# An encoder layer's output projection: its steps issued in the program's order on every engine, with outputs, gates and C stored by chunk

## The chip, the cores and the metric

The kernel runs on one core of one Trainium2 chip. The metric is the time of one execution in microseconds (us), and the median of several executions is what is compared: 2937.86 us before, from three runs between 2935.85 and 2945.36 us.

## What is computed

One layer of a bidirectional encoder in float32, for two sequences of 1024 and 2048 tokens with 1024 features each. An RMS norm and an input projection feed a Fourier group (512 features) and a bidirectional state-space group (1536 features, in chunks of 128 tokens). Each has a SiLU gate. The state-space outputs are normalised in four groups of 384 features, all 2048 features pass one output projection, and the residual is added:

```
y_s = y_s * jax.nn.silu(z_s)
yg = y_s.reshape(b, s, N_BC_GROUPS, D_SSM // N_BC_GROUPS)
yg = yg * lax.rsqrt(jnp.mean(yg * yg, axis=-1, keepdims=True) + EPS)
y_s = yg.reshape(b, s, D_SSM) * ssd_norm_w
h = h + jnp.concatenate([y_f, y_s], axis=-1) @ w_out
h = h + (p @ w_ple_in) * jax.nn.sigmoid(h @ w_ple_gate)
```

A final RMS norm closes the layer. The change touches the output projection (`h + ... @ w_out`) and the group norm ahead of it.

## The kernel before

Four phases follow one another. The first, the input projection with the state-space part, takes about two thirds of the span; its order is written out by hand. The second does the Fourier group, the third the output projection, the fourth the gated embedding and the last norm. The order of the last three is made by a scheduler that lists the instructions of all engines ahead of time.

The 3072 tokens are three blocks of eight chunks of 128 tokens (P, S1, S2). The first two phases leave their outputs in device memory: `Yd`, for each block 16 rows of 128 features by 1024 tokens; `ZSd`, the gates of block S1; `CTd`, its matrices C. In these arrays the tokens of one feature lie together, so that the rows of one chunk are 512 B pieces.

The output projection takes 24 steps: twelve pairs of chunks for the first 1024 of the 2048 features (p = 0, rows 0 to 7 of `Yd`), then the same twelve for the others (p = 1). The partial result goes to `Hd` in between. A step is a Strassen-Winograd product: 256 tokens by 1024 features times 1024 by 1024 weights as seven products P1 to P7 of quarter size. The left operands are A11, A12, A22, S1, S2, S3, S4, sums and differences of quarters of `y` (`halves`, lines 1066 to 1097: `s1`, `s2`, `s3` and last `s4`). Each operand is split into a high part `ah` (ACT, a cast, L1074) and a low part `al` (DVE, a subtraction, L1075); each product is twelve matmuls of 512 columns (L1104). P1, P6 and P7 accumulate one after another in the same PSUM bank X; after each of them ACT copies the bank to a buffer `pu` (L1113; the copies are called p1, u2, u3). P2 writes bank Y, P5 and P3 bank Z, P4 bank W. DVE adds banks Y, Z and W to the residual `ht` (L1218), POOL adds the copies (L1219). Weights come from `WSd`, 1 MB for each product and each half of the features, and are split like the operands (`product_weights`, L858 on ACT, L859 on DVE).

Ahead of that stands the preparation of a step (`prepare`): the loads of `y` (SyncE); in steps 4 to 7 and 16 to 19, whose chunks are in block S1, a correction for the backward state (matmuls `po` L1185, products on DVE L1186, sums on POOL L1190); squares on ACT (L865) and their sums `rs` on POOL (L866, L867) for each chunk; the split of `rs` into `sh` (ACT L871, POOL L872); two matmuls `pb` that add over the features (L874); Ln and Exp on ACT, each after a table load (L875, L876); and the scaling of `y` on POOL (L880). The program writes down the preparation of step n+2, then the scaling and operands of step n+1, then the products of step n, and the scheduler interleaves them.

## Time and profile before

| what | value |
|---|---|
| median of three runs | 2937.86 us |
| the profiled execution | 2937.68 us |
| its span, first to last instruction | 2935.9 us |
| mean granted TensorE clock | 0.983 |
| mean DMA rate | 150 GB/s |

The profile is that of one execution. Busy time is given for TensorE's matmuls (PE) and weight loads (PEld), VectorE (DVE), ScalarE (ACT) and GpSimd (POOL); SP is SyncE, which issues DMAs. A group's row has its line, engine, operation, tiles (out<-in) and count, then the busy time in us and the mean in ns, then the engine's idle time just before and who ended it. A row of the timeline has a start and a duration in us; a bracket at its end has the idle time before it and what ended that. Matmuls overlap in the pipeline, so their durations are longer than the distance between their starts. A wait for several events is put down to the one that came last.

### The profile page before, as it was taken

The numbers are of one execution on the slowest core, as the hardware profiler recorded it, in microseconds if no ns is written. First come the engines' busy times: TensorE is split into PE (matmuls) and PEld (weight loads), VectorE is DVE, ScalarE is ACT, GpSimd is POOL, SyncE is SP. The second block draws the span as 40 slices with busy tenths as digits, with TensorE's granted clock in tenths as the row PEclk, the third lists the DMA queues.
The fourth block names the chain that finished last, engine by engine and source line by source line (L and its number), as shares of the span: only waits on it lengthen the run. The fifth ranks groups of instructions, "written<-read, shape, count | busy, mean of one in ns | idle before, by whom it ended". The sixth has DMA issues, their size and how long they took to land.

```text
span 2935.9 us, 46306 instructions
## 1 busy us (share of the span) xinstructions
PE 2806.0 (96%) x17206; PEld 2550.2 (87%) x17206; DVE 2148.7 (73%) x3364; ACT 1454.0 (50%) x3008; POOL 1497.0 (51%) x1091
## 2 busy tenths in 40 slices
PE   6999999999999999999999999788998899989998
PEld 6999999999999999999999999776776677768887
DVE  3787777687778686778787776796767876776665
ACT  4545465443545564445444444345555645555554
POOL 1255656542567777643656655455777577610000
PEclk9999999999999999999999999889999999999999
DMA  3244565462465665544455554466453654451221
GB/s 96 88 146 150 166 187 166 125 185 79 127 192 165 200 189 159 160 123 117 144 161 157 154 159 132 151 231 227 144 173 127 229 167 141 158 198 67 96 96 63
DMA packets 327997, 440.09 MB, mean 150 GB/s; under 512 B 19824, under 2 KB 250932, under 8 KB 323932
## 3 DMA queue, kind: packets, MB, share of 16 engines
q1 hardware_dynamic: 327484, 436.08, 47.1%
q8 instruction: 136, 2.23, 0.3%
q10 hardware_dynamic: 288, 1.05, 0.1%
q14 instruction: 89, 0.73, 0.1%
HBM read 328.41 MB, written 109.71 MB: 149 GB/s over the span
## 4 chain that ended last, share of the span: by engine, by line
PE 73%; DVE 7%; POOL 6%; issue 5%; DMA 5%; ACT 4%; SPq 0%; POOLq 0%; DVEq 0%; ACTq 0%
PE ps L361 41%; PE X L1104 7%; PE Z L1104 4%; PE po L648 4%; PE pst L606 3%; PE pd L574 3%; PE W L1297 2%; PE Y L1104 2%; DMA y<-Yd 2%; PE ptt L421 1%; DVE s L1080 1%; DVE al L1075 1%; PE W L1104 1%; PE pr L1028 1%; POOL wl L190 1%
## 5 line engine op out<-in xcount | busy, mean ns | idle before, releaser
L361 PE MATMUL ps<-uh,wh 128*128 128x342 f32 (+1 forms) x2880 | 955.8, 332 | 11.4 <-ACT uh L267 8.2
L361 PE MATMUL ps<-ul,wh 128*128 128x342 f32 (+1 forms) x2880 | 920.6, 320 | 2.5 <-DVE ul L268 2.5
L361 PE MATMUL ps<-uh,wl 128*128 128x342 f32 (+1 forms) x2880 | 922.2, 320 | 0.4 <-POOL wl L190 0.4
L190 POOL TENSOR_TENSOR wl<-wr,wh 128x1024 fp32r<-128x1024 f32 x120 | 296.4, 2470 | 659.3 <-ACT wh L189 658.1
L361 PEld LDWEIGHTS ps<-uh,wh 128*128 128x128 f32 x2880 | 545.6, 189 | 35.0 <-issue 15.8
L361 PEld LDWEIGHTS ps<-ul,wh 128*128 128x128 f32 x2880 | 548.5, 190 | 4.2 <-DVE ul L268 3.5
L361 PEld LDWEIGHTS ps<-uh,wl 128*128 128x128 f32 x2880 | 545.1, 189 | 1.2 <-POOL wl L190 1.1
L558 ACT ACTIVATE R<-R,lb 128x128 f32<-128x128 f32 x1152 | 352.8, 392 | 16.9 <-POOL R L549 16.9
L549 POOL TENSOR_SCALAR_AFFINE_SELECT R<-R 128x512 f32<-128x512 f32 x288 | 275.7, 980 | 6.8 <-DMA R<-ROWd 6.8
L586 POOL TENSOR_TENSOR xw<-xm,wd 128x512 f32<-128x512 f32 x144 | 189.5, 1327 | 136.3 <-ACT xm L423 110.8
L617 DVE SCALAR_TENSOR_TENSOR H<-H,cd,pst 128x64 f32<-128x64 f32 x888 | 182.6, 274 | 102.2 <-PE pst L606 100.0
L367 ACT COPY raw<-ps 128x342 f32<-128x342 f32 x180 | 79.1, 439 | 340.6 <-PE ps L361 339.7
L1104 PE MATMUL X<-whP,ah 128*128 128x512 f32 x480 | 196.7, 410 | 14.1 <-ACT pu L1113 8.4
L402 DVE SCALAR_TENSOR_TENSOR xT<-raw,cvt,xT 128x1024 f32<-128x1024 f32 x144 | 195.5, 1358 | 2.6
L1104 PE MATMUL X<-wlP,ah 128*128 128x512 f32 x480 | 194.5, 405 | 1.6 <-DVE wlP L859 1.6
L1104 PE MATMUL X<-whP,al 128*128 128x512 f32 x480 | 193.6, 403 | 2.4 <-DVE al L1075 2.4
L1219 POOL TENSOR_TENSOR ht<-ht,pu 128x512 f32<-128x512 f32 x96 | 150.4, 1578 | 72.3 <-ACT pu L1113 46.6
L652 DVE TENSOR_TENSOR y<-y,yt 128x512 f32<-128x512 f32 (+1 forms) x144 | 161.4, 1121 | 5.0
L272 ACT ACTIVATE zT<-ps 128x342 f32<-128x342 f32 (+1 forms) x108 | 49.1, 455 | 220.7 <-PE ps L361 220.4
L1075 DVE TENSOR_TENSOR al<-s,ah 128x512 fp32r<-128x512 f32 x144 | 137.7, 981 | 26.5 <-ACT ah L1074 26.0
L565 DVE TENSOR_TENSOR R<-R,cb 128x512 f32<-128x512 f32 x144 | 148.5, 1031 | 5.0
L651 DVE TENSOR_TENSOR yt<-po,er 128x512 f32<-128x512 f32 (+1 forms) x144 | 91.2, 633 | 75.9 <-PE po L648 67.7
(266 smaller groups left out, 5772.8 us busy)
## 6 DMA issues: line engine op xcount, KB each, us to landing
R<-ROWd SPq DMA_DIRECT2D x144, 512.0 KB
wr<-in_w_in SPq DMA_DIRECT2D x120, 512.0 KB
er<-EXPd SPq DMA_DIRECT2D x144, 256.0 KB
Hd<-ht SPq DMA_DIRECT2D x48, 512.0 KB
ht<-Hd SPq DMA_DIRECT2D x48, 512.0 KB
y<-Yd SPq DMA_DIRECT2D x46, 512.0 KB
wlP<-WSd SPq DMA_DIRECT2D x21, 1024.0 KB
Yd<-y SPq DMA_DIRECT2D x72, 256.0 KB
```

What stands on the lines that cost most here:

```text
L190: G.tensor_tensor(wl, raw, wh.bitcast(F32), op=ALU.subtract)
L361: T.matmul(ps[:, :n], lhsT=wt[:, kt, :], rhs=ut[:, kt, :n], start=(i == 0), stop=(i == 3 * KT - 1))
L402: V.scalar_tensor_tensor(dst, raw[:, k:k + TB], cvt[:, 20 * k + ct:20 * k + ct + 1], dst, op0=ALU.mult, op1=ALU.add)
L549: G.affine_select(out=R, in_=R, pattern=[[0, 2], [0, 2], [sgn, P]], compare_op=ALU.is_ge, fill=NEG, base=0, channel_multiplier=-sgn)
L558: S.activation(R[:, h, d, c, :], R[:, h, d, c, :], AF.Exp, bias=self.B.lb[:, 2 * p + c, hc + h:hc + h + 1])
L565: V.tensor_tensor(E[0], E[0], cb.unsqueeze(1).broadcast_to([P, 2, 2 * P]), op=ALU.mult)
L586: G.tensor_tensor(xw, self.xm[c4].rearrange("p c (h e) -> p c h e", h=2), col(self.B.wd[:, c4:c4 + 4, hc:hc + 2]).broadcast_to([P, 4, 2, 6 ...
L617: V.scalar_tensor_tensor(dst[:, e], H[d][:, cc, e], B.cd[:, cc, hc + h:hc + h + 1], pst[:, c, e], op0=ALU.mult, op1=ALU.add)
L652: V.tensor_tensor(y[:, cr], y[:, cr], t[:, cr], op=ALU.add)
L1075: V.tensor_tensor(al, src, ah.bitcast(F32), op=ALU.subtract)
L1104: T.matmul(ps, lhsT=at[:, k, :], rhs=wt[:, k, :], start=(first and i == 0), stop=(i == 11), skip_group_check=not first)
L1219: return lambda t: G.tensor_tensor(h, h, t, op=ALU.add)
```

## The change

Four things change.

- `Yd`, `ZSd` and `CTd` are laid out by chunk: the rows of one chunk lie together. A load of `y` for one chunk is then 4 KB in one piece for each partition, not eight of 512 B; the stores by the first two phases, for several chunks at a time, are in pieces of 512 B, not of 2 or 4 KB.
- The preparation and the products are cut into the small methods of a class `Step`, and a function `run(n)` writes them down in a fixed order: the products of step n (`c`), between them the roots, scaling and operands of step n+1 (`d`), and the loads, corrections, squares and the split of the sums of step n+2 (`e`). For runs 1 to 22 the scheduler is off: every engine takes its instructions in the order of the program. Runs 0 and 23, the preparation of step 1 and all else stay with the scheduler.
- `big`, the buffer of the correction, is taken anew for each corrected step; before, one was kept throughout.
- In run 11, the last of the first half, the weights of the second half are asked for after each product and split at fixed places (`weights_asked`, `weights_parted`). Before, `product_weights` stood behind the step.

The diff, cut to its core (lines left out are marked):

```diff
-    Yd = [dram.tile([P, 16, TB], F32, name=f"Yd{i}") for i in range(3)]
...
-    ZSd = dram.tile([P, NU, TB], F32, name="ZSd")
-    CTd = dram.tile([P, NG, TB], F32, name="CTd")
+    ZSd = dram.tile([P, NCH, NU, P], F32, name="ZSd")
+    CTd = dram.tile([P, NCH, NG, P], F32, name="CTd")
...
-                        pre(s_ + 9, nc.sync.dma_start, CTd[:, i, :], CT)
+                        pre(s_ + 9, nc.sync.dma_start, CTd[:, :, i, :], CT.rearrange("p (c l) -> p c l", l=P))
...
-                nc.sync.dma_start(Yd[self.B.bi][:, unit_place(self.u), tk], self.y[c4].rearrange("p c l -> p (c l)"))
+                cs = slice(c4, c4 + 4)
+                nc.sync.dma_start(Yd[self.B.bi][:, cs, unit_place(self.u), :], self.y[c4])
                 if self.B.b["n"] == "S1":
-                    nc.sync.dma_start(ZSd[:, self.u, tk], self.zT[:, tk])
+                    nc.sync.dma_start(ZSd[:, cs, self.u, :], self.zT[:, tk].rearrange("p (c l) -> p c l", l=P))
...
-    def group_rstd(sh, pb, rs):
+    def group_parts(sh, rs):
         S.copy(sh[:, 0], rs)
         G.tensor_tensor(sh[:, 1], rs, sh[:, 0].bitcast(F32), op=ALU.subtract)
+    def group_rstd(sh, pb, rs):
         for j in range(2):
             T.matmul(pb, lhsT=ones_r, rhs=sh[:, j], start=(j == 0), stop=(j == 1))
         S.activation(rs, pb, AF.Ln, bias=eps4, scale=1.0 / 384.0)
@@ -938,7 +941,7 @@
...
-        first_y = [Yd[0][:, 0:8, q * P:q * P + P] for q in range(2)]
+        first_y = [Yd[0][:, q, 0:8, :] for q in range(2)]
...
-                    Yd[seq + q][:, fourier_place(f), :], yv[:, q * TB:(q + 1) * TB])
+                    Yd[seq + q][:, :, fourier_place(f), :], yv[:, q * TB:(q + 1) * TB].rearrange("p (c l) -> p c l", l=P))
...
-        def prepare(p, i):
...
+        steps = [(p, i) for p in range(2) for i in range(NP)]
...
+        class Step:
...
-                    nc.sync.dma_start(y, Yd[bi][:, 8 * p:8 * p + 8, tk])
+                    nc.sync.dma_start(y, Yd[bi][:, c, 8 * p:8 * p + 8, :])
...
+                        nc.sync.dma_start(self.big[:, q, 0:2, :], CTd[:, c, 2 * p:2 * p + 2, :])
+                        nc.sync.dma_start(self.big[:, q, 2:8, :], ZSd[:, c, 6 * p:6 * p + 6, :])
...
+            def correct(self, q):
...
+                for g in range(2):
+                    po = mps.tile([P, 3, P], F32, tag="sm", bufs=3, name="po")
+                    for j in range(3):
+                        T.matmul(po[:, j, :], lhsT=hbs[-1][:, 3 * g + j, :], rhs=ct[:, g, :], start=True, stop=True)
+                    V.tensor_tensor(zb[:, 3 * g:3 * g + 3, :], po, zb[:, 3 * g:3 * g + 3, :], op=ALU.mult)
+                ssd = self.ys[q].rearrange("p (r k) l -> p r k l", r=2)[:, :, 1:4, :]
+                G.tensor_tensor(ssd, ssd, zb.rearrange("p (r k) l -> p r k l", r=2), op=ALU.add)
...
+            def squared(self, q):
...
+                squares(self.ys[q], sq, self.rss[q])
+            def summed(self):
+                self.sh = yp.tile([P, 2, 4, P], F32R, tag="sh", bufs=1, name="sh")
+                group_parts(self.sh, self.rs)
+            def rooted(self):
                 pb = mps.tile([P, 4, P], F32, tag="sm", bufs=3, name="pb")
-                group_rstd(sh, pb, rs)
-            def rest():
-                for q in range(2):
-                    if rss:
-                        group_scale(ys[q], rss[q])
-                    bi, c = todo[2 * i + q]
+                group_rstd(self.sh, pb, self.rs)
+            def scaled(self, q):
+                if not self.first:
+                    group_scale(self.ys[q], self.rss[q])
...
+            def operand(self, k):
+                a11, a12, a21, a22 = (self.ys[q][:, 4 * r:4 * r + 4, :] for q in range(2) for r in range(2))
+                if k == 0:
+                    self.two("A11", a11)
+                    self.diff("s3", a11, a21, ALU.subtract)
+                elif k == 1:
+                    self.diff("s1", a21, a22, ALU.add)
+                    self.two("A12", a12)
+                elif k == 2:
+                    self.diff("s2", self.s1, a11, ALU.subtract)
+                    self.two("S2", self.s2)
+                elif k == 3:
+                    self.two("S1", self.s1)
+                elif k == 4:
+                    self.two("S3", self.s3)
+                elif k == 5:
+                    self.two("A22", a22)
+                elif "S4" not in self.A:
+                    self.diff("s4", a12, self.s2, ALU.subtract)
+                    self.two("S4", self.s4)
+            def add(self, q, ns, ps):
+                h = self.hts[q][:, ns]
                 V.tensor_tensor(h, ps, h, op=ALU.add)
-                return lambda t: G.tensor_tensor(h, h, t, op=ALU.add)
+            def plus(self, q, ns, t):
+                h = self.hts[q][:, ns]
+                G.tensor_tensor(h, h, t, op=ALU.add)
+            def stored(self):
...
+        def weights_parted(w):
...
+        def run(n, newer=None):
...
+            c.operand(6)
+            product(X, c.A, W_, "A11", "P1")
+            if d is not None and not d.first and n:
+                d.rooted()
             p1 = kept(X)
-            product(Y, A, W, "A12", "P2")
-            add(0, N0, Y)(p1)
-            product(X, A, W, "S2", "P6", first=False)
+            if e is not None:
+                if steps[n + 2] == (1, 0):
+                    incoming(1)
+                e.rows()
+            if d is not None:
+                d.scaled(0)
+                d.scaled(1)
+            product(Y, c.A, W_, "A12", "P2")
+            asked(0)
+            c.add(0, N0, Y)
+            c.plus(0, N0, p1)
+            if b is not None:
+                b.stored()
+            product(X, c.A, W_, "S2", "P6", first=False)
+            asked(1)
             u2 = kept(X)
-            product(Z, A, W, "S1", "P5")
-            more = add(1, N1, Z)
-            product(X, A, W, "S3", "P7", first=False)
+            if d is not None:
+                d.operand(0)
+            product(Z, c.A, W_, "S1", "P5")
+            asked(2)
+            c.add(1, N1, Z)
+            if d is not None:
+                d.operand(1)
+                d.operand(2)
+            if e is not None:
+                e.correct(0)
+            parted(0)
+            product(X, c.A, W_, "S3", "P7", first=False)
+            asked(3)
             u3 = kept(X)
-            more(u3)
-            product(X2, A, W, "A22", "P4")
-            add(1, N0, X2)(u3)
-            product(Z, A, W, "S4", "P3", first=False)
-            add(0, N1, Z)(u2)
-            for q, (bi, c) in enumerate(todo[2 * i:2 * i + 2]):
-                nc.sync.dma_start(Hd[bi * NCH + c], hts[q])
-        ready = prepare(0, 0)()
+            c.plus(1, N1, u3)
+            if e is not None:
+                e.correct(1)
+                e.squared(0)
+            if d is not None:
+                d.operand(3)
+            parted(1)
+            product(X2, c.A, W_, "A22", "P4")
+            asked(4)
+            c.add(1, N0, X2)
+            c.plus(1, N0, u3)
+            if d is not None:
+                d.residuals()
+                d.operand(4)
+            if e is not None:
+                e.squared(1)
+            parted(2)
+            product(Z, c.A, W_, "S4", "P3", first=False)
+            asked(5)
+            c.add(0, N1, Z)
+            if e is not None:
+                e.summed()
+            if d is not None:
+                d.operand(5)
+            c.plus(0, N1, u2)
+            parted(3)
+            if newer is not None:
+                asked(6)
+                for k in range(4, 7):
+                    parted(k)
+                W.update(new)
+        all_[0].rows()
+        for k in range(7):
+            all_[0].operand(k)
+        all_[0].residuals()
         ld = product_weights(0, NAMES[3:4], W)
         with tc.issue_after(ld.ins):
-            coming = prepare(0, 1)
+            all_[1].rows()
+        for q in range(2):
+            all_[1].squared(q)
+        all_[1].summed()
+        all_[1].rooted()
         ld = product_weights(0, NAMES[4:], W)
         with tc.issue_after(ld.ins):
             incoming(0)
-        steps = [(p, i) for p in range(2) for i in range(NP)]
-        for n, (p, i) in enumerate(steps):
-            cur, after = ready, coming
-            with tc.issue_after(ld.ins):
-                if n + 2 < len(steps):
-                    if steps[n + 2] == (1, 0):
-                        incoming(1)
-                    coming = prepare(*steps[n + 2])
-                if n + 1 < len(steps):
-                    ready = after()
-                else:
-                    ph.close()
-                    q4 = ctx.enter_context(tc.tile_pool(name="q4", bufs=1, **R_))
-                    ready = turned(0)
-            outputs(i, W, *cur)
-            if i == NP - 1:
-                W = {}
-                last_w = product_weights(p + 1, NAMES, W)
+            run(0)
+        with tc.manual_schedule():
+            for n in range(1, len(steps) - 1):
+                run(n, newer=W if n == NP - 1 else None)
+        c = all_[-1]
+        c.operand(6)
+        ph.close()
+        q4 = ctx.enter_context(tc.tile_pool(name="q4", bufs=1, **R_))
+        ready = turned(0)
+        all_[-2].stored()
+        X, Y, Z, X2 = bank("X"), bank("Y"), bank("Z"), bank("W", bufs=2)
+        product(X, c.A, W, "A11", "P1")
+        p1 = kept(X)
+        product(Y, c.A, W, "A12", "P2")
+        c.add(0, N0, Y)
+        c.plus(0, N0, p1)
+        product(X, c.A, W, "S2", "P6", first=False)
+        u2 = kept(X)
+        product(Z, c.A, W, "S1", "P5")
+        c.add(1, N1, Z)
+        product(X, c.A, W, "S3", "P7", first=False)
+        u3 = kept(X)
+        c.plus(1, N1, u3)
+        product(X2, c.A, W, "A22", "P4")
+        c.add(1, N0, X2)
+        c.plus(1, N0, u3)
+        product(Z, c.A, W, "S4", "P3", first=False)
+        c.add(0, N1, Z)
+        c.plus(0, N1, u2)
+        c.stored()
+        W = {}
+        last_w = product_weights(2, NAMES, W)
```

What this does to the order of the instructions, at three places. First PE, at the matmuls `pb` of a step with no correction. Before, they stand between the products, wherever the scheduler put them, here after a product into X and among the first matmuls of one into Z:

```order
L1104 MATMUL X<-whP_23618,ah 128x512
L1104 MATMUL X<-wlP_23619,ah 128x512
L1104 MATMUL X<-whP_23618,al 128x512
L874 MATMUL pb<-sh,ones_r 128x512
L1104 MATMUL Z<-whP_23651,ah 128x512
L1104 MATMUL Z<-wlP_23652,ah 128x512
L874 MATMUL pb<-sh,ones_r 128x512
L1104 MATMUL Z<-whP_23651,al 128x512
```

Now they stand in every step between P1 (into X) and P2 (into Y):

```order
L1108 MATMUL X<-whP_23490,ah 128x512
L1108 MATMUL X<-wlP_23491,ah 128x512
L1108 MATMUL X<-whP_23490,al 128x512
L877 MATMUL pb<-sh,ones_r 128x512 x2
L1108 MATMUL Y<-whP_23509,ah 128x512
L1108 MATMUL Y<-wlP_23510,ah 128x512
```

So P2 and all that follows is queued behind `pb`. Second ACT, from the copy `sh` of the sums to the roots. Before, in the second half (`s` are sums and differences, `pu` a copy of bank X):

```order
L871 CAST sh<-rs 128x512
L1074 CAST ah<-s_22983 128x512
L1074 CAST ah<-s_22981 128x512
L1074 CAST ah<-s_22979 128x512
L1113 COPY pu<-X 128x512
L875 ACT_TABLE_LOAD
L875 ACTIVATE rs<-pb,eps_117 128x512
L1074 CAST ah<-y 128x512
L876 ACT_TABLE_LOAD
L876 ACTIVATE rs<-rs 128x512
```

Now, in every step; the first cast is that of A22 of the next step, the second that of its S4, and the copy at the end is p1 (and u2 behind it):

```order
L871 CAST sh<-rs 128x512
L1239 CAST ah<-y 128x512
L1239 CAST ah<-s_22028 128x512
L878 ACT_TABLE_LOAD
L878 ACTIVATE rs<-pb,eps_117 128x512
L879 ACT_TABLE_LOAD
L879 ACTIVATE rs<-rs 128x512
L1117 COPY pu<-X 128x512 x2
```

Before, a copy of bank X stood ahead of the first table load; now p1 stands behind the second root, and the cast of S4 ahead of the first load. Third POOL, from the scaling of one step to that of the next, with no correction. Now:

```order
L883 TENSOR_TENSOR y<-y,rs 128x2x384 x2
L1271 TENSOR_TENSOR ht<-ht,pu 128x512 x2
L867 TENSOR_TENSOR rs<-sq 128x256
L868 TENSOR_TENSOR rs<-rs,sq 128x256
L1271 TENSOR_TENSOR ht<-ht,pu 128x512
L867 TENSOR_TENSOR rs<-sq 128x256
L868 TENSOR_TENSOR rs<-rs,sq 128x256
L872 TENSOR_TENSOR sh<-rs,sh 128x512
L1271 TENSOR_TENSOR ht<-ht,pu 128x512
```

Before, for one such step:

```order
L880 TENSOR_TENSOR y<-y,rs 128x2x384 x2
L866 TENSOR_TENSOR rs<-sq 128x256
L1219 TENSOR_TENSOR ht<-ht,pu 128x512
L867 TENSOR_TENSOR rs<-rs,sq 128x256
L866 TENSOR_TENSOR rs<-sq 128x256
L867 TENSOR_TENSOR rs<-rs,sq 128x256
L1219 TENSOR_TENSOR ht<-ht,pu 128x512
L872 TENSOR_TENSOR sh<-rs,sh 128x512
L1219 TENSOR_TENSOR ht<-ht,pu 128x512 x2
```

The first sums of squares of a step stood right behind the scaling of the step ahead of it; now two additions of `pu` stand in front of them, the second of which takes u3, the copy after P7.

More of the change, by code (lines that the diff above doesn't have):

```diff
@@ L66, in col @@
         return t.unsqueeze(len(t.shape))
-    Yd = [dram.tile([P, 16, TB], F32, name=f"Yd{i}") for i in range(3)]
+    Yd = [dram.tile([P, NCH, 16, P], F32, name=f"Yd{i}") for i in range(3)]
     UFd = [dram.tile([P, NF, n], F32, name=f"UFd{i}") for i, n in enumerate((1024, 2048))]
@@ new lines, in weights_parted @@
+        def weights_parted(w):
+            wh, wl = w
+            raw = wl.bitcast(F32)
+            for k in range(4):
+                S.copy(wh[:, k, :], raw[:, k, :])
+                V.tensor_tensor(wl[:, k, :], raw[:, k, :], wh[:, k, :].bitcast(F32), op=ALU.subtract)
+        all_ = [Step(n) for n in range(len(steps))]
+        def run(n, newer=None):
+            c = all_[n]
+            b = all_[n - 1] if n else None
+            d = all_[n + 1] if n + 1 < len(steps) else None
+            e = all_[n + 2] if n + 2 < len(steps) else None
+            m = c.p + 1
+            W_, new = dict(W), {}
+            asked = lambda k: new.update({NAMES[k]: weights_asked(m, NAMES[k])}) if newer is not None else None
+            parted = lambda k: weights_parted(new[NAMES[k]]) if newer is not None else None
```

84 lines of the change are left out of this document (44 added, 40 removed).

## The prediction

> **What bounds the kernel now.** I read the page, then the output projection by itself: its stretch by engine, the two matmuls that mark its ends, who keeps TensorE (PE) waiting there, and the mean duration of each operation. Over the whole span PE is the busiest engine:
>
> ```profile
> PE 2806.0 (96%) x17206; PEld 2550.2 (87%) x17206; DVE 2148.7 (73%) x3364; ACT 1454.0 (50%) x3008; POOL 1497.0 (51%) x1091
> ```
>
> The change rewrites only the projection. Product P2 is the only one that writes bank Y, so its first matmul marks a step. Step 1 and step 23 have theirs here; the third row is the stretch between (busy us and count of PE, PEld, DVE, ACT, POOL, then clock, DMA share, GB/s):
>
> ```profile
> 2047.91 0.46 PE L1104 MATMUL Y<-whP,ah 128*128 128x512 f32 x1
> 2557.10 0.40 PE L1104 MATMUL Y<-whP,ah 128*128 128x512 f32 x1
> ...
> 2047.91:2557.10 509.19, 476.21 (x2047) 374.87 (x2047) 379.50 (x396) 264.74 (x399) 365.19 (x254) 0.97 0.49 161
> ```
>
> So 22 steps take 509.2 us, 23.1 us each. What PE needs follows from the chain of waits, where a product of twelve matmuls passes in 2.80 us, and from the correction matmuls, 25.1 us in 8 steps (3.1 us each):
>
> ```profile
> 2383.11 2.80 PE X L1104 x12
> ...
> L1185 PE MATMUL po<-big,hb 128*128 128x128 f32 x192 | 25.1, 274 | 0.0
> ```
>
> Seven products and two sum matmuls (2 x 0.233) are 20.1 us a step, 23.2 us in the 8 steps with a correction. The stage therefore stands some 40 us above PE's own work: waits of 33 us in all, and a lower clock behind them. Of the eleven rows of PE's waits (us in total, times, longest), the first two and the last:
>
> ```profile
> PE W L1104 <- ACT ah L1074: 7.7, 6, 2.9
> PE Z L1104 <- DVE ht L1218: 6.3, 3, 3.7
> ...
> PE pb L874 <- ACT sh L871: 0.3, 1, 0.3
> ```
>
> No wait is steady: even the first row has 6 in 22 steps. The scheduler has interleaved steps so that PE nearly always has another product. That is the most there is to win.
>
> **The change part by part: the loop.** In the new order each engine runs its list strictly in order, and every step is the same. I look for a chain that leads from one operation of a step to the same one of the next; its length is the step's period if it exceeds 20.1 us. Means of the stretch (line, engine, operation, count; busy us, mean ns):
>
> ```profile
> L871 ACT CAST sh<-rs 128x512 fp32r<-128x512 f32 x22 | 13.6, 619 | 27.6 <-POOL rs L867 27.6
> L1074 ACT CAST ah<-y 128x512 fp32r<-128x512 f32 x66 | 39.8, 613 | 20.6 <-PE X L1104 9.5 <-POOL y L880 7.7 <-PE Z L1104 2.2
> L1075 DVE TENSOR_TENSOR al<-y,ah 128x512 fp32r<-128x512 f32 x68 | 79.2, 1169 | 61.8 <-ACT ah L1074 61.7
> L1080 DVE TENSOR_TENSOR s<-y,s 128x512 f32<-128x512 f32 x22 | 31.7, 1442 | 0.5
> L875 ACT ACT_TABLE_LOAD x22 | 28.2, 1283 | 0.4
> L875 ACT ACTIVATE rs<-pb,eps 128x512 f32<-128x512 f32 x22 | 15.2, 690 | 5.3 <-PE pb L874 5.0
> L876 ACT ACT_TABLE_LOAD x22 | 28.2, 1283 | 0.4
> L876 ACT ACTIVATE rs<-rs 128x512 f32<-128x512 f32 x22 | 13.9, 633 | 0.2
> L1113 ACT COPY pu<-X 128x512 f32<-128x512 f32 x62 | 35.9, 578 | 8.2 <-PE X L1104 8.2
> L1219 POOL TENSOR_TENSOR ht<-ht,pu 128x512 f32<-128x512 f32 x83 | 130.4, 1582 | 35.9 <-ACT pu L1113 24.9 <-DVE ht L1218 4.6 <-ACT ah L1074 2.6
> L866 POOL TENSOR_TENSOR rs<-sq 128x256 f32<-128x256 f32 x44 | 40.6, 923 | 40.7 <-ACT sq L865 38.5 <-DMA Hd<-ht 2.1
> L867 POOL TENSOR_TENSOR rs<-rs,sq 128x256 f32<-128x256 f32 x44 | 46.5, 1058 | 2.4
> ```
>
> Start where POOL finishes the sums of squares of step n+2 (`rs`). Then, in order: ACT copies `sh` (0.62) and, next in its list, casts A22 of step n+1 (0.61); DVE subtracts for A22 (1.17) and forms s4 (1.44), for which ACT casts S4 (0.62); only behind that cast stand the first table load (1.28), Ln (0.69), the second load (1.28), Exp (0.63) and the copy p1 of bank X (0.58). P6 accumulates onto X and must wait for p1. P6, P5 and P7 follow (8.40), then u3 (0.58); POOL adds u3 (1.58), makes the first chunk's sums (0.92 + 1.06), adds u3 to the other half (1.58) and makes the second chunk's sums (1.98). That is the start again, one step later. Without rounding the sum is 25.0 us.
>
> Eleven hand-overs come on top. One takes 0.07 us: the copy ends at 2379.61 and POOL starts at 2379.68.
>
> ```profile
> 2378.99 0.62 ACT L871 CAST sh<-rs 128x512 fp32r<-128x512 f32 x1 [1.73 <-POOL rs L867]
> ...
> 2379.68 1.28 POOL L872 TENSOR_TENSOR sh<-rs,sh 128x512 fp32r<-128x512 f32 x1 [0.73 <-ACT sh L871]
> ```
>
> I take 0.8 us together, so 25.8 us, with PE idle twice a step: before `pb` (it waits for the low half of `sh`, then P2 is queued behind it) and about 3 us before P6. The clock makes the second one dearer. After a wait of 2.43 us the old trace has eight matmuls 0.42 us apart, not 0.23:
>
> ```profile
> 2185.65 0.50 PE L1104 MATMUL X<-whP,ah 128*128 128x512 f32 x1 [2.43 <-ACT pu L1113]
> ...
> 2186.46 0.60 PE L1104 MATMUL X<-whP,ah 128*128 128x512 f32 x1
> ...
> 2189.84 0.41 PE L1104 MATMUL X<-wlP,ah 128*128 128x512 f32 x1
> ```
>
> They take 3.38 us, not 1.87: 1.5 us lost, 1.6 with the slow first one, and P6 and P5 lie in the loop. My gap may shrink to about 2.4 us if contention is mild, so I charge half, 0.8 us: **26.6 us** a step. The Trainium skill ("TensorE: Matmul & The Clock Gate", "Why this matters for your kernels") asks for no idle gaps above about 3 us, one idle window before the clock halves; by that my gap would lie on the edge. The trace, with 2.43 us, is stricter. Without any slow clock the forecast would be 16 us lower (0.8 x 20 steps).
>
> In the eight steps with a correction (n = 2 to 5, 14 to 17) the chain runs another way, through POOL's two correction adds:
>
> ```profile
> L1186 DVE TENSOR_TENSOR big<-po,big 128x384 f32<-128x384 f32 x32 | 17.2, 548 | 15.2 <-PE po L1185 11.8 <-POOL ht L1219 3.3
> L1190 POOL TENSOR_TENSOR y<-y,big 128x768 f32<-128x768 f32 x16 | 32.9, 2056 | 20.3 <-DVE ht L1218 10.1 <-DMA y<-Yd 4.6 <-DVE big L1186 3.6
> L1218 DVE TENSOR_TENSOR ht<-Z,ht 128x512 f32<-128x512 f32 x44 | 29.9, 680 | 11.5 <-PE Z L1104 10.0 <-DMA ht<-Hd 1.3
> ```
>
> From `rs` through p1 it is the same, 8.9 us; then P6 and P5 5.60; on DVE the add of Z 0.68, four operand operations at 0.68 (POOL is idle there) with one cast 0.62, and two products 1.10; on POOL 2.06, 1.58, 2.06, 1.98, 1.58, 1.98. Together 30.9, with hand-overs 31.8 us.
>
> **Weights of the second half.** Run 11 now also holds 28 casts and 28 subtractions, in fixed places, 16 of each between the operands A22 and S4, inside the chain:
>
> ```profile
> L859 DVE TENSOR_TENSOR wlP<-wlP,whP 128x512 fp32r<-128x512 f32 x28 | 23.8, 901 | 0.7 <-ACT whP L858 0.7
> ```
>
> 16 x 0.90 = 14.4, so run 11 takes 41 us. Run 1 takes 21, since the sums it needs were made ahead.
>
> **The layouts.** A load of `y` becomes 128 pieces of 4 KB instead of 1024 of 512 B, the stores the reverse. For the same 512 KB the old trace has 5.98 us in small pieces and 3.41 in large:
>
> ```profile
> 2058.54 5.98 DMA y<-Yd
> 2438.35 3.41 DMA ht<-Hd
> ```
>
> The faster loads gain nothing: in the new order `y` is asked for when s4 is done, and its squares follow u3, by the sum above 14 us later. On SyncE they now stand ahead of the stores of step n-1 and the residuals of n+1; those are needed only after P2 of the next step. The slower stores run under the first phase's products, which hardly wait for anything:
>
> ```profile
> L361 PE MATMUL ps<-uh,wh 128*128 128x342 f32 (+1 forms) x2880 | 955.8, 332 | 11.4 <-ACT uh L267 8.2
> ```
>
> If that cover were gone, 96 stores of 256 KB at 1.3 us more each would cost 125 us; nothing in the row points to it. In the Fourier phase, where `yv` has one buffer, I charge 3 us (bounds 0 and 12 stores x 2.6 = 31).
>
> **Sum.** 12 x 26.6 + 8 x 31.8 + 21 + 41 = 635.6 us against 509.2: +126.4, with the stores +129.4. The profiled execution took 2937.68 us, 1.7 over its span and equal to the median of the runs within 0.2. Forecast: **3067 us**.
>
> **Rivals.** (1) My means contain waits for the port that DVE and POOL share, which might not recur. The shortest of each:
>
> ```profile
> L1075 DVE TENSOR_TENSOR al<-y,ah x68: 674/1082/2337, 2047.3 to 2553.3; 128x512 fp32r<-128x512 f32 x68
> L1080 DVE TENSOR_TENSOR s<-y,s x22: 676/1666/1787, 2056.2 to 2541.7; 128x512 f32<-128x512 f32 x22
> L1219 POOL TENSOR_TENSOR ht<-ht,pu x83: 1273/1720/1801, 2049.5 to 2550.4; 128x512 f32<-128x512 f32 x83
> ```
>
> A22's subtraction then saves 0.50, s4 0.77, the two adds 0.62, and the two pairs of sums, at the shortest (718 and 734 ns), 1.06: the loop is 22.9 us, the corrected one, with 0.45 off its correction adds, 28.4, and run 11 takes 37: 560 us, **2988** without the stores' 3. Chance 0.13. (2) Full blocking every time: DVE's operation at 2527.73 ends 0.54 us after POOL's at 2528.97, so it stood still until then.
>
> ```profile
> 2527.22 1.75 POOL L1219 TENSOR_TENSOR ht<-ht,pu 128x512 f32<-128x512 f32 x1
> 2527.73 1.78 DVE L1080 TENSOR_TENSOR s<-y 128x512 f32<-128x512 f32 x1
> ```
>
> If each of the chain's four such operations takes about 1.8 us (+0.63, +0.36, +0.22, +0.22) and the clock is slow in every step (+0.8), the periods are 28.6 and 33.2, run 11 takes 44: 674 us, with the stores **3105**. Chance 0.15. The Trainium skill ("SBUF — State Buffer", "Who interferes with whom") states that rule, a DVE operation with two SBUF inputs against a POOL operation that reads SBUF; these rows agree. (3) The other side: the pipeline does what a pipeline promises, every operand is ready, PE is the bound, 12 x 20.1 + 8 x 23.2 + 20 + 34 = 481 us, **2909**. It decides if the loop is under 20.1 us; the shortest rows leave it 2.8 us above, and it would need `pb` not to hold P2 and p1 not to stand behind Exp. Chance 0.05. (4) The gain and the loss cancel, or the new order isn't kept: a loop of 21.2 us, **2938**. The rows of the order speak against it; 0.03.
>
> **How the numbers follow.** The forecast's own case has 0.64. The range 2988 to 3105 spans rivals 1 and 2 and leaves out 3, 4 and what of rival 2 lies above its value, about half: 0.15 together. A difference of 0.3% (9 us) is what a measurement of this kernel can tell. Faster 0.05, same 0.03, slower 0.92.
>
> **What would show it.** Bank Y's first matmuls 26 to 27 us apart in plain steps and about 32 in corrected ones; PE waiting once a step for `sh` before `pb` and once for `pu` before X, 20 times each, 1.5 to 3.5 us; ACT waiting for `rs` before `sh`; a PE share near 0.8 and a clock below 0.97 in the stretch. It is wrong if PE's waits are few, or if the period is under 22 us; if POOL has no idle time in a step, POOL and not the loop is the bound.

## The result and the profile after

The changed kernel takes **3066.02 us** (median of 4 runs, 3061.7 to 3068.48) against 2939.33 us of the kernel before on the same chip (2935.85 to 2945.36): ratio 1.0436, 95% interval 1.0421 to 1.045, slower by some 127 us. The profiled execution has a span of 3062.9 us, 127.0 above that of before.

The first matmuls of bank Y, which mark the steps, and the stretch from step 1 to step 23 (columns as in the prediction):

```profile
2060.73 0.63 PE L1108 MATMUL Y<-whP,ah 128*128 128x512 f32 x1
2698.33 0.39 PE L1108 MATMUL Y<-whP,ah 128*128 128x512 f32 x1
...
2060.73:2698.33 637.60, 521.97 (x2072) 406.12 (x2070) 297.03 (x387) 264.51 (x398) 334.58 (x252) 0.90 0.40 131
```

22 steps take 637.6 us, not 509.2, and PE is busy for 82% of it at a clock of 0.90. PE's waits in nearly the same stretch (2053 to 2680), the whole list where there were eleven small rows before:

```profile
PE X L1108 <- ACT pu L1117: 74.3, 20, 11.1
PE pb L877 <- ACT sh L871: 25.6, 10, 6.1
PE pb L877 <- POOL sh L872: 18.3, 22, 0.9
```

Two waits, one before P6 in 20 steps and one before the group sum's matmuls (`pb`). In a plain step the second is only the 0.85 us for the low half of `sh`; of the ten longer ones, for ACT's copy, eight stand in the corrected steps, one before step 1's mark and one in run 11. One plain step of the timeline shows why:

```profile
2287.79 0.62 ACT L871 CAST sh<-rs 128x512 fp32r<-128x512 f32 x1 [1.93 <-POOL rs L868]
2288.32 0.61 ACT L1239 CAST ah<-y 128x512 fp32r<-128x512 f32 x1
2288.96 1.34 DVE L1240 TENSOR_TENSOR al<-y,ah 128x512 fp32r<-128x512 f32 x1 [2.38 <-ACT ah L1239]
2289.71 1.74 POOL L1271 TENSOR_TENSOR ht<-ht,pu 128x512 f32<-128x512 f32 x1
2289.81 0.50 PE L877 MATMUL pb<-sh,ones_r 128*128 128x512 f32 x1 [0.85 <-POOL sh L872]
2290.23 1.77 DVE L1233 TENSOR_TENSOR s<-y,s 128x512 f32<-128x512 f32 x1
2292.09 0.62 ACT L1239 CAST ah<-s 128x512 fp32r<-128x512 f32 x1 [3.16 <-DVE s L1233]
2292.73 1.28 ACT L878 ACT_TABLE_LOAD   x1
2294.02 0.69 ACT L878 ACTIVATE rs<-pb,eps 128x512 f32<-128x512 f32 x1
2294.73 1.28 ACT L879 ACT_TABLE_LOAD   x1
2296.02 0.63 ACT L879 ACTIVATE rs<-rs 128x512 f32<-128x512 f32 x1
2296.56 0.57 ACT L1117 COPY pu<-X 128x512 f32<-128x512 f32 x1
2297.18 0.50 PE L1108 MATMUL X<-whP,ah 128*128 128x512 f32 x1 [4.08 <-ACT pu L1117]
...
2303.57 0.69 DVE L1233 TENSOR_TENSOR s<-y 128x512 f32<-128x512 f32 x1
...
2307.67 0.58 ACT L1117 COPY pu<-X 128x512 f32<-128x512 f32 x1
...
2308.33 1.31 POOL L1271 TENSOR_TENSOR ht<-ht,pu 128x512 f32<-128x512 f32 x1 [6.76 <-ACT pu L1117]
...
2309.61 1.21 POOL L867 TENSOR_TENSOR rs<-sq 128x256 f32<-128x256 f32 x1
2310.90 1.20 POOL L868 TENSOR_TENSOR rs<-rs,sq 128x256 f32<-128x256 f32 x1
```

Read the brackets downwards: each engine waits for the one above it. ACT waits 3.16 us for s4 with the roots queued behind it, although the second `pb` matmul starts at 2289.81; p1 is last in that list, so PE waits 4.08 us for it; POOL then waits 6.76 us for u3 before it can add and sum. The next copy of `sh` comes at 2314.90, 27.11 us after this one.

The spacing of the marks, from the first matmuls of bank Y in both timelines (us; run n is the one from mark n to n+1):

```
                          before           after     predicted
step 0 to 1                 29.6            42.8     (no change)
plain steps (11)            15 to 26        22.7 to 27.8, mean 26.4     26.6
corrected (8)               19 to 28        30.1 to 32.6, mean 31.5     31.8
run 1                       25.8            23.6     21
runs 11 and 12 together     49.7            71.5     41 + 26.6
1 to 23 (22 steps)         509.2           637.6     635.6
23 to the end              378.8           364.6     (no change)
```

Seven of the plain steps take 27.1 us. Three are shorter: the two right behind corrected ones (25.3 us), and run 22 (22.7 us), whose end is marked early, since the scheduler, which orders step 23, put its first bank-Y matmul ahead of P1.

### The profile page after: what moved, and what is told of

It reads as the page before. It is cut to its first block, busy times and chain, and to the rows that moved or that the text cites. A ratio compares the mean times of both kernels' runs of the same rounds, so it can differ in the third digit from the quotient of the medians.

```text
span 3062.9 us, 46116 instructions
## 1 busy us (share of the span) xinstructions
PE 2848.4 (93%) x17206; PEld 2578.1 (84%) x17206; DVE 2071.8 (68%) x3364; ACT 1455.0 (48%) x3008; POOL 1469.7 (48%) x1091
## 5 line engine op out<-in xcount | busy, mean ns | idle before, releaser
L1108 PE MATMUL X<-whP,ah 128*128 128x512 f32 x480 | 207.1, 432 | 80.1 <-ACT pu L1117 78.6
L1240 DVE TENSOR_TENSOR al<-y,ah 128x512 fp32r<-128x512 f32 x69 | 63.2, 917 | 235.2 <-ACT ah L1239 235.2
L1108 PE MATMUL X<-wlP,ah 128*128 128x512 f32 x480 | 202.8, 423 | 1.7 <-DVE wlP L860 1.7
L1108 PE MATMUL X<-whP,al 128*128 128x512 f32 x480 | 201.1, 419 | 0.9 <-DVE al L1240 0.9
L1271 POOL TENSOR_TENSOR ht<-ht,pu 128x512 f32<-128x512 f32 x96 | 139.6, 1456 | 127.3 <-ACT pu L1117 98.9
L1108 PEld LDWEIGHTS X<-whP,ah 128*128 128x128 f32 x480 | 97.2, 203 | 113.0 <-ACT pu L1117 88.9
```

The lines of the kernel that those rows point to most:

```text
L1108: T.matmul(ps, lhsT=at[:, k, :], rhs=wt[:, k, :], start=(first and i == 0), stop=(i == 11), skip_group_check=not first)
L1271: G.tensor_tensor(h, h, t, op=ALU.add)
```

## The experiments

The theory: the order that every engine now keeps ties a step to the one before it by one chain (group sums, A22, s4, S4, roots, p1, P6 to u3, sums), and that chain's length is the period. The rivals: the new layouts cost time; or the steps are long because DVE and POOL hold each other up, wherever an operation stands. The experiments ran on three chips, on which the kernel before took 2935.81, 2937.37 and 2936.99 us; ratios are to that kernel on the same chip, differences from the changed kernel are to its 3066.02 us.

**1. The layouts alone**, in the old kernel:

```diff
-    Yd = [dram.tile([P, 16, TB], F32, name=f"Yd{i}") for i in range(3)]
+    Yd = [dram.tile([P, NCH, 16, P], F32, name=f"Yd{i}") for i in range(3)]
...
-                    nc.sync.dma_start(y, Yd[bi][:, 8 * p:8 * p + 8, tk])
+                    nc.sync.dma_start(y, Yd[bi][:, c, 8 * p:8 * p + 8, :])
```

(and the same for `ZSd` and `CTd` and their stores).

> The old kernel with nothing changed but the three layouts by chunk (Y, gates, C): the pieces of the stores are 512 B and those of the loads 4 KB, and the scheduler still sets the order. Theory (the fixed order costs all of the 127 us, the layouts nothing): 2936 to 2943 us, and the first Y-bank matmul of step 0 within 1 us of the old 2018.3. Rival (the small stores lengthen the first two phases, hidden in the changed kernel by something else): up to 31 us more, 2970 us, with that matmul later by as much. A gain of more than 5 us would say that the old order waited for the loads of y.

Measured: 2933.08 us against 2935.81, ratio 0.9986 (0.9976 to 0.9997). Step 0 begins 2.4 us earlier than the 2018.30 of before:

```profile
2015.93 0.40 PE L1105 MATMUL Y<-whP,ah 128*128 128x512 f32 x1
```

These 2.4 us mean little: in the profiles of eight kernels with these layouts and the changed kernel's start (the changed one and experiments 2, 3, 5 to 7, 9 and 10) the same mark lies between 2017.40 and 2020.17. The layouts cost nothing; by the interval of the ratio they gain 1 to 7 us.

**2. The scheduler's order back**, all else as changed:

```diff
-        with tc.manual_schedule():
+        with tc.issue_after(ld.ins):
             for n in range(1, len(steps) - 1):
                 run(n, newer=W if n == NP - 1 else None)
```

> The changed kernel with one thing undone: the steps 1 to 22 are not pinned to the program's order, the scheduler orders them as it did before. Layouts, the new step code, the fixed places of the weight loads and of the stores stay as written. Theory (the order that is kept is the cost): about 2940 us, 2925 to 2955, Y-bank firsts no longer at a steady 27.1 us, PE's waits for pu and for sh gone. Rival (the new code itself, its buffers and its places for weights and stores, costs): 3000 us or more.

Measured: 2953.39 us, ratio 1.0058 (1.004 to 1.0076). The stretch from step 1 to 23:

```profile
2048.10:2571.61 523.51, 479.08 (x2048) 378.14 (x2048) 375.34 (x396) 266.01 (x399) 365.80 (x254) 0.96 0.46 156
```

Keeping the order costs 3066.0 - 2953.4 = 112.6 us. The rest, 18 us over the old kernel, belongs to the new code under the scheduler: against experiment 1 the 22 steps are 523.5 - 503.7 = 19.8 us longer, 8.3 of it in runs 4 to 10, 6.8 in runs 11 and 12 with the weights, 4.8 behind them. What costs them was not looked into.

**3. p1 ahead of the roots:**

```diff
+            p1 = kept(X)
             if d is not None and not d.first and n:
                 d.rooted()
-            p1 = kept(X)
```

> The changed kernel with one line moved: ACT copies p1 ahead of the two roots of the next step, so that P6 no longer stands behind a table load, Ln, a table load and Exp (1.28 + 0.69 + 1.28 + 0.63 = 3.88 us a step). Theory (P6 stands in the loop behind the roots): the wait before P6 shrinks by 3.9 us; the loop then closes through POOL (roots, two scalings of up to 3.6 together, the add of p1, the add of u3, the sums), which by its own rows is about 24.7 us in a plain step. 12 x 2.4 + 8 x 1.5 to 3.9 = 41 to 60 us less, 3006 to 3025 us. Rival (PE loses the time to the port that DVE and POOL share, or to the clock): less than 10 us, over 3055 us.

Measured: 3031.64 us, ratio to the old kernel 1.0321 (1.0302 to 1.0341), 34 us less than the changed kernel; plain steps 25.2 to 25.7, corrected ones 30.1 to 30.4. PE's waits between 2053 and 2640:

```profile
PE pb L877 <- ACT sh L871: 40.0, 18, 7.9
PE po L1201 <- DVE big L1202: 24.4, 8, 3.5
PE pb L877 <- POOL sh L872: 15.6, 21, 0.9
PE X L1108 <- ACT pu L1117: 9.0, 6, 8.2
```

The wait for `pu` is nearly gone (9.0 us, not 74.3), and the waits for `sh` and for the corrections take its place: the loop closes another way, as expected. The gain was put too high, 41 to 60 us: the plain steps are 25.2 us or more, not 24.7, and the corrected ones gain 1.3 us, not 1.5 to 3.9.

**4. The same operations in another fixed order.** The new program order of a step; c is step n, d n+1, e n+2; `ad` and `pl` are the adds of DVE and POOL for the bank (Z1 and Z2: after P5 and P3; X2 is bank W), ROOT is Ln and Exp of d, SC the scalings, A11 to S4 the casts and subtractions of an operand, s1 to s3 the sums and differences, Q the squares and sums of e, SH the split of those sums, CO the corrections of e, ROWS, ST and RES the DMAs of y, stores and residuals:

```diff
-S4(c) P1 PB ROOT p1 ROWS SC0 SC1 P2 adY plY ST P6 u2 A11 s3 P5 adZ1 s1 A12 s2 S2 CO0
-P7 u3 plZ1 CO1 Q0 S1 P4 adX2 plX2 RES S3 Q1 P3 adZ2 SH A22 plZ2
+P1 PB p1 ROOT SC0 ROWS P2 P6 adY SC1 ST plY CO0 CO1 A12 P5 adZ1 u2
+P7 A11 s3 P4 s1 s2 Q0 u3 P3 S3 Q1 adX2 A22 SH plX2 S4(d) adZ2 RES plZ1 S2 S1 plZ2
```

> The changed kernel with the same operations in another fixed order: PE's products stand as they do, but ACT copies p1 ahead of the roots; POOL takes the sums of squares of step n+2 between the adds of u3's halves or ahead of them and the adds late; S4 of step n+1 is formed at the end of step n; the corrections come right after P6; three weights of the second half are split in run 12. Theory (only the loop's order costs; with no chain from one step to the next longer than PE's own work, PE is the bound): 20.1 to 20.6 us plain and 23.2 to 24 corrected, so 14 x 20.4 + 8 x 23.6 = 474 us for the 22 steps against 637.6, 2905 us (2890 to 2935). Rival (DVE and POOL hold each other up at their port, whatever the order; 15 us of POOL and about 20 of DVE a step when slowed): 23 us and more a step, 2960 us or more.

Measured: **2911.05 us**, ratio 0.9912 (0.9891 to 0.9933): faster than both kernels. Plain steps 20.06 us, corrected ones 22.73; between 2086 and 2277 PE has no wait at all. From step 1 to 23:

```profile
2064.36:2545.30 480.94, 472.07 (x2093) 382.41 (x2092) 348.18 (x389) 265.77 (x397) 380.27 (x253) 0.98 0.50 174
```

DVE and POOL are busier than in the changed kernel (348 and 380 us against 297 and 335, in 157 us less). They must run at the same time for at least 348 + 380 - 481 = 247 us, and PE waits for 9.6 us in all. In this order the port is not the bound; the order was. What is left over PE's own work lies mostly at step 0 to 1 (42.6 us) and at the weights of runs 11 and 12 (23.9 and 31.3).

**5. No table loads:**

```diff
-        S.activation(rs, pb, AF.Ln, bias=eps4, scale=1.0 / 384.0)
-        S.activation(rs, rs, AF.Exp, scale=-0.5)
+        S.activation(rs, pb, AF.Identity, bias=eps4, scale=1.0 / 384.0)
+        S.activation(rs, rs, AF.Copy, scale=-0.5)
```

> The changed kernel with the roots replaced: Identity (pb / 384 + eps) and Copy (times -0.5) on ACT in place of Ln and Exp, so that the two table loads of a step go; the outputs are not the normalised ones. Theory (the loads lie in the loop): 2 x 1.28 = 2.57 us less a step, 22 steps, 56 us: 3010 us. The wait before P6 then falls from 4.1 to about 1.5 us; if with it the slow clock behind it goes, up to 1.5 us a step more, 2977 us. Rival (the loads are hidden beside DVE's s4 and PE's P2): 3066 us.

Measured: 2980.05 us, ratio 1.0152 (1.0136 to 1.0168), 86 us less; plain steps 22.88, 4.24 less. ACT's rows in one step, and P6's first matmul:

```profile
2287.59 0.62 ACT L1239 CAST ah<-s 128x512 fp32r<-128x512 f32 x1 [3.16 <-DVE s L1233]
2288.12 0.68 ACT L878 ACTIVATE rs<-pb,eps 128x512 f32<-128x512 f32 x1
2288.83 0.63 ACT L879 ACTIVATE rs<-rs 128x512 f32<-128x512 f32 x1
2289.37 0.57 ACT L1117 COPY pu<-X 128x512 f32<-128x512 f32 x1
2289.99 0.50 PE L1108 MATMUL X<-whP,ah 128*128 128x512 f32 x1 [1.39 <-ACT pu L1117]
```

P6 now waits 1.39 us, not 4.08, and its matmuls follow each other at 0.23 us. So 2.57 us are the loads, and the other 1.67 fit the slow clock that followed the long wait (1.6 us, below). The total is near the 2977 us given for that case.

**6 and 7. The same cast three times over, on the chain and off it:**

```diff
-                S.copy(ah, src)
+                for _ in range(3 if name == "S4" else 1):
+                    S.copy(ah, src)
```

with `"A12"` in place of `"S4"` in the second.

> The changed kernel with one cast of every step made three times over, the cast of S4, which stands in the loop in front of the roots: the two more take 0.52 us each (three in a row take 1.66 us, one 0.62). Theory: 1.04 x 22 = 23 us more, 3089 us (3084 to 3092). Rival (the steps are long because the engines are busy and share ports, not because of the chain): the same as with the cast of A12 made three times.

> The changed kernel with the cast of A12 made three times over in every step, the same work on the same engine, but at a place where ACT waits 3.7 us for DVE's s2 right behind it and the subtraction that needs it comes 2.4 us later. Theory: nothing, 3064 to 3069 us. Rival (ACT's load or the port counts): as much more as with S4, some 20 us.

Measured: with S4 3111.2 us, ratio 1.0598 (1.058 to 1.0615), 45 us more than the changed kernel; with A12 3065.18 us, 1.0436 (1.0417 to 1.0455), the changed kernel's own. The casts and the wait behind them with S4:

```profile
2311.26 1.92 ACT L1240 CAST ah<-s 128x512 fp32r<-128x512 f32 x3 [3.16 <-DVE s L1233]
...
2317.64 0.80 PE L1108 MATMUL X<-whP,ah 128*128 128x512 f32 x1 [5.38 <-ACT pu L1117]
```

The pair tells the theories apart: equal work on the same engine costs 45 us in one place and nothing in the other. The size for S4 was missed, 45 us instead of 23. Into one destination the casts take 1.92 us, not 1.66, so the wait grows by 1.3 us (22 x 1.3 = 29), and behind 5.38 us the clock is slow for 8 or 13 matmuls in turn, so plain steps take 28.5 and 29.5 us.

**8. The start of the reordered kernel.** Step 0 too in a fixed order, with y of step 1 asked for ahead of the four weights still to come:

```diff
...
+        all_[1].rows()
+        for name in NAMES[3:]:
+            W[name] = weights_asked(0, name)
+        incoming(0)
         with tc.manual_schedule():
-            for n in range(1, len(steps) - 1):
+            for n in range(len(steps) - 1):
```

and in run 0: squares of step 1 behind p1, one weight split after ROWS, PB, SC1 and A11 each, the roots after the second of them.

> The reordered kernel (2911 us) with its start mended: step 0 too is kept in a fixed order, y of step 1 is asked for ahead of the four weights that still have to come, its squares and roots stand between the splits of those weights, and the last three weights of the second half are split a product apart in run 12. In the reordered kernel the Y-bank firsts of steps 0 and 1 stand 42.6 us apart, since the roots of step 1 end at 2047.8 and the group sums of step 2 are late for the product matmuls behind them; PE's own work there is 22.7 us, the 16 splits of weights about 11 us of DVE. Theory: 25 to 32 us there instead of 42.6, 2894 to 2904 us in all. Rival (the weights' loads and splits set the start): no change, 2909 to 2913 us. A start in a fixed order could also be worse, if ACT waits for the loads of the weights with work behind it.

Measured: 2909.1 us (2902.28 to 2910.94), ratio 0.9903 (0.9888 to 0.9919): not to be told from experiment 4. Step 0 to 1 falls from 42.6 to 34.9 us, short of the 25 to 32; but step 0 begins 1.6 us later, and runs 11 to 13 together take 77.2 us, not 75.2.

**9. S4 behind p1**, in the changed kernel:

```diff
-            c.operand(6)
             product(X, c.A, W_, "A11", "P1")
             if d is not None and not d.first and n:
                 d.rooted()
             p1 = kept(X)
+            c.operand(6)
```

> The changed kernel with one line moved: s4 is formed and S4 cast behind the roots and p1, not in front of them. In the changed kernel ACT waits 3.16 us for DVE's s4 and casts S4 before the first table load may start, though pb is there 1.5 us after the cast of A22. Theory (the order of ACT's list makes the loop): the roots and p1 end 3.3 us earlier; the wait before P6 falls from 4.08 to 0.8 us, and with it the slow clock behind it, 1.6 us: 22.2 us in a plain step, and 1.5 to 4.9 less in a corrected one, 12 x 4.9 + 8 x 1.5 to 4.9: 2968 to 2995 us. Rival (s4's 1.77 us beside POOL is lost wherever it stands, as DVE and POOL share the port): less than 25 us, over 3040 us.

Measured: 2966.77 us, ratio 1.0103 (1.0086 to 1.012): **99 us less by one line**. One step:

```profile
2237.50 0.62 ACT L1239 CAST ah<-y 128x512 fp32r<-128x512 f32 x1
2238.13 1.28 ACT L878 ACT_TABLE_LOAD   x1
2239.41 1.78 DVE L1233 TENSOR_TENSOR s<-y,s 128x512 f32<-128x512 f32 x1
...
2242.07 0.57 ACT L1117 COPY pu<-X 128x512 f32<-128x512 f32 x1
...
2242.54 0.62 ACT L1239 CAST ah<-s 128x512 fp32r<-128x512 f32 x1
2242.69 0.51 PE L1108 MATMUL X<-whP,ah 128*128 128x512 f32 x1 [0.41 <-ACT pu L1117]
```

The table load follows A22's cast at once, P6 waits 0.41 us, plain steps take 21.9 us and corrected ones 26.8 to 27.4. The time is 1 us under the range of 2968 to 2995.

**10. Both moves, p1, roots, S4:**

```diff
-            c.operand(6)
             product(X, c.A, W_, "A11", "P1")
+            p1 = kept(X)
             if d is not None and not d.first and n:
                 d.rooted()
-            p1 = kept(X)
+            c.operand(6)
```

> The changed kernel with both moves, p1 first, then the roots, then S4. If the two moves shorten two different waits their gains add, 34 us from p1 and what S4 alone gave. Theory: they don't add, since with either one the loop closes through the roots, the two scalings, the adds and the sums on POOL; with p1 ahead and the roots 3.3 us earlier that loop is 25.2 - 3.3 = 21.9 us in a plain step, still above PE's 20.1: about as S4 alone, 2955 to 2985 us, with PE waiting for pb and hardly for pu.

Measured: 2969.35 us, ratio 1.0111 (1.0096 to 1.0126), plain steps 22.1 to 22.8 us. PE's waits between 2053 and 2590:

```profile
PE pb L877 <- ACT sh L871: 31.9, 16, 6.1
PE pb L877 <- POOL sh L872: 18.3, 22, 0.9
...
PE X L1108 <- ACT pu L1117: 1.8, 1, 1.8
```

As expected: the gains do not add. With the wait for `pu` gone PE waits before `pb`, which fits the loop through the roots, the scalings and the sums; no experiment cut a link of that loop alone.

**11. The reordered kernel's weights piece by piece** (the edit against experiment 8), run 0 mended once more (P5 ahead of PB, p1's add behind the group sum's low half; the 28 splits of runs 11 and 12 one at a time between other items):

```diff
-    PARTS = [(0, 'P7'), (1, 'P4'), (2, 'P3'), (3, 'plZ2')]
+    PARTS = [(0, 'u2', 0), (0, 'P7', 1), (0, 'A11', 2), (0, 's3', 3), (1, 'P4', 0), ...]
```

> The reordered kernel with the fixed start once more: in step 0 POOL makes the low half of the group sum before it adds p1, and P5 stands in front of the group sum's matmuls (PE waited 6.4 us for them); the 28 splits of the second half's weights stand one by one between the other work of runs 11 and 12, not four in a row. Theory: step 0 to 1 falls from 34.9 to about 27 us and runs 11 to 13 from 77.2 to about 68 us: 2890 to 2898 us. Rival (DVE has no room for 28 splits beside two steps: 28 x 0.7 to 0.9 = 20 to 25 us): no gain there, 2900 to 2905 us.

Measured: 2906.35 us (2904.97 to 2907.27), ratio 0.9896 (0.9881 to 0.9911); both gains failed to come. Step 0 to 1 is 34.7 us and runs 11 to 13 take 78.3. PE's first waits between 2015 and 2062, and that stretch:

```profile
PE W L1108 <- DVE wlP L1288: 2.0, 2, 1.4
PE Z L1108 <- ACT whP L1287: 1.9, 1, 1.9
...
2015.00:2062.00 47.00, 38.06 (x129) 26.80 (x128) 40.75 (x41) 29.43 (x48) 30.20 (x20) 0.85 0.61 231
```

DVE is busy for 40.8 of 47 us there, and 5.1 of PE's 8.8 us of waits are for splits of weights (`wlP`, `whP`). That speaks for the rival of experiment 8, that the weights set the start. For runs 11 to 13 the rival given here, no room on DVE, is not shown: DVE is busy for 62.3 of the 78.3 us, and PE waits there 5.2 us for `sh`, 5.0 for copies of bank X and 0.8 for the weights.

## Why the prediction was right, point by point

- **The loop.** Right, and shown from both sides: work added on the chain costs (6), beside it not (7); a link taken out or moved shortens the step (5, 9); and with the same operations in an order without it the steps are PE's own 20.06 and 22.73 us (4), near the 20.1 and 23.2 of the prediction. It named all links in their order.
- **Its length.** 27.1 us in the steady steps against 26.6; with the shorter ones named under the table the mean of the eleven plain steps is 26.4. The terms were off both ways: A22's subtraction 1.34 (1.17 charged) and s4 1.77 (1.44); the adds of u3 1.31 and 1.30 (1.58 each); the sums 2.41 and 1.46 (1.98 each); the slow clock 1.6 (0.8). Together +0.65, about the 0.5 seen.
- **The clock.** The half that was charged was the mis-sized term: P6's wait came out at 4.08 us, not the 2.4 to 3 that the charge went by, and the full 1.6 us were lost in the plain steps. Experiment 5 has the other size: in its plain steps none is lost behind 1.39 us.

Rows of one P6, the first slow matmul, the last, and the first of P5 (start, us):

```profile
2298.32 0.63 PE L1108 MATMUL X<-wlP,ah 128*128 128x512 f32 x1
...
2301.31 0.47 PE L1108 MATMUL X<-whP,al 128*128 128x512 f32 x1
2301.62 0.40 PE L1108 MATMUL Z<-whP,ah 128*128 128x512 f32 x1
```

The slow stretch lasts 3.3 us and begins 1.1 us after the wait has ended. The Trainium skill ("TensorE: Matmul & The Clock Gate", "What's actually happening") describes windows of 3.4 us that run free of the kernel, with half the clock after an idle one; the length agrees, while the longer stretches of experiment 6 (13 matmuls, some 5.5 us) are more than one window. By that rule the loss behind a gap depends on where the gap falls, as in experiment 6, where it alternates.

- **Rivals 1 and 2 (the port).** Between the two: s4 is slow as in rival 2 (1.77 us beside a POOL add of 1.74; s3, of the same shape and also with two inputs, takes 0.69 at 2303.57 with POOL idle), the adds of u3 are as short as in rival 1. The Trainium skill's rule ("SBUF — State Buffer", "Who interferes with whom"), that a DVE operation with two SBUF inputs and a POOL operation that reads SBUF exclude each other, agrees with the s4 row. Experiment 9 shows what it is worth: s4 still takes 1.78 us there, but the roots no longer wait for it. Rival 2's sum has a slip: its own terms make 28.8 us a plain step, not 28.6, and some 3 us more in all.
- **Rival 3 (PE-bound).** Wrong for this order, right for another: experiment 4 measured 2911 us and 480.9 for the 22 steps, where the prediction had 2909 and 481. Its two conditions, `pb` not holding P2 and p1 not behind Exp, were two of several: with p1 moved alone the loop closes elsewhere (3), and the dearest single item was s4 and S4's cast in front of the roots (9), which the prediction had in its chain but did not name as the place to cut.
- **Corrected steps.** Mean 31.5 against 31.8, and by the path named. In the step from 2507.34 POOL's first correction add waits for DVE's products, which stand behind the operands:

```profile
2523.79 2.25 DVE L1202 TENSOR_TENSOR big<-po,big 128x384 f32<-128x384 f32 x4
2524.88 1.84 POOL L1204 TENSOR_TENSOR y<-y,big 128x768 f32<-128x768 f32 x1 [6.33 <-DVE big L1202]
```

No experiment cut this part of the chain by itself.

- **Weights and run 1.** Runs 11 and 12 took 71.5 us against 67.6, run 1 23.6 against 21: 6.5 us too little. The plain and corrected steps together came out 4.5 us shorter than charged, about what run 22's early mark takes off, so that the sum for the 22 steps was only 2.0 us too small.
- **The signs.** The spacing, the share of PE (0.82) and the clock (0.90) came as named. PE was to wait 20 times for `sh` for 1.5 to 3.5 us: it did so 10 times, and not in the steady plain steps. The 20 waits for `pu` came, but at 4.1 us in the steady plain steps.
- **The layouts.** Charged 3 us; experiment 1 has -1 to -7.
- **What the sum left out.** It compared the 22 steps between two marks and took the rest as unchanged. But a mark does not stand for the same finished work in both kernels. Step 0 to 1 became 13.2 us longer: PE runs 89 matmuls in it, not 77, and waits for the sums of step 2:

```profile
2058.80 0.80 PE L877 MATMUL pb<-sh,ones_r 128*128 128x512 f32 x1 [6.09 <-ACT sh L871]
```

From step 23 to the end it became 14.2 us shorter. Both stretches (columns as above):

```profile
2557.10:2935.90 378.80, 360.72 (x1657) 290.26 (x1655) 242.65 (x379) 197.71 (x378) 14.99 (x10) 0.98 0.30 107
2698.33:3062.90 364.57, 351.72 (x1621) 283.30 (x1619) 236.01 (x377) 193.24 (x371) 10.30 (x6) 0.99 0.31 109
```

Before, 36 more matmuls, three products' worth, were still to do behind step 23's mark: 8.4 us at 2.80 a product. PE's waits in the stretch fell from 9.0 to 3.5 us. Together that is 13.9 of the 14.2.

So the span grew by 128.4 + 13.2 - 14.2 - 0.3 (step 0's mark itself) = 127.1 us. That the total came within a microsecond is in part luck: the two shifts of the marks cancel, and the steps' 2.0 us too little stand against 3 us charged for stores that cost nothing.

## What to carry to other kernels

Where every engine keeps the program's order, follow one operation round to itself a step later, with all that is queued between on each engine, and compare that length with the bounding engine's work; an operand that nobody needs yet, formed and cast in front of roots that everybody waits for, cost 99 us here. An order kept by hand is not slower in itself: with no loop longer than PE's work it beat the scheduler by 25 us. When steps are compared between marks, check that a mark means the same amount of finished work in both kernels.

## What the runs showed of the hardware that was not expected

Three casts in a row into one destination took 1.92 us (6); into three destinations, in the reordered kernel, 1.66:

```profile
2253.37 1.66 ACT L1239 CAST ah<-s 128x512 fp32r<-128x512 f32 x3 [0.53 <-DVE s L1233]
```

Behind the waits of 4.06 to 4.08 us in the changed kernel 7 to 11 matmuls were slow, mostly 8. Behind 5.37 or 5.38 us in experiment 6 it was 8 or 13 in turn in most plain steps, so that the price of a gap differs by 1 us from one step to the next. The length of the wait alone does not decide: the kernel before lost some 1.6 us behind 2.43 us, and the changed kernel none behind this one:

```profile
2514.10 0.51 PE L1108 MATMUL X<-whP,ah 128*128 128x512 f32 x1 [2.74 <-ACT pu L1117]
```
